# RWKV wave of a hybrid decoder step: fewer state DMAs, earlier loads, another order of the output groups, the last item and the last norms

## The chip, the cores and the metric

One core of one Trainium2 chip runs the whole step as one program. The metric is the device time of one execution in microseconds (us); the kernel before was run three times, and one further execution was profiled. Engines: PE (TensorE), ACT (ScalarE), DVE (VectorE), POOL (GpSimd) and SP (SyncE), which in this kernel issues every DMA.

## What is computed

Two layers for 1104 tokens (64 sample tokens in 8 sequences, 16 meta tokens, 1024 prompt tokens): a gated DeltaNet layer, which the change doesn't touch, then an RWKV-7 layer, a residual add and a final RMSNorm. The RWKV layer carries one state S per head (16 heads, 64 x 64) through the tokens:

```python
S = (S * d_t[:, :, None, :]
     + jnp.einsum('bhvk,bhk->bhv', S, -kk_t)[..., None] * b_t[:, :, None, :]
     + v_t[..., None] * k_t[:, :, None, :])
y_t = jnp.einsum('bhvk,bhk->bhv', S, r_t)
...
y = (y - mean) * lax.rsqrt(var + GN_EPS) * lnx_w + lnx_b      # per head
y = y + jnp.sum(r_h * k_h * r_k, -1, keepdims=True) * v_h
out = (y.reshape(B, T, D) * jax.nn.silu(z)) @ w_o
x = x + out                                                    # residual
y_out = rmsnorm(x, final_norm_w)
```

The eight sample sequences each start from a state of their own (`state_rwkv`) and return their new one (`s_rwkv`); the prompt's last state is `p_rwkv`.

## The kernel before, in words

Everything up to the wave is done by 1836 us: the DeltaNet layer, the RWKV projections, and the inverse "systems" of each chunk, written to DRAM (`ttd`).

The **wave** (lines 1864 to 1981) works on 24 **items**: 3 segments of 384, 384 and 336 tokens times 8 head pairs; item n is segment n // 8, pair n % 8, and has six chunks of 64 tokens. Step `tau` of the wave runs chunk `tau - 2n` of each live item n, so three items are in flight, one enters every two steps, and item n occupies steps 2n to 2n + 5. A step is: `step_solve` (PE products with the states, then the ACT copy `X`, line 1499, which opens the step in the profile's views here), `step_inner` (PE products with the system tile `rTT`, then two ACT copies), `step_old`, `step_state` (PE updates `rS` and `rY`, DVE writes the state), `y_stats`. PE and ACT run in the order in which the program writes their instructions (`manual_schedule`); DVE, POOL and SP are ordered by the planner of the framework, each in one queue.

Between these, a step places other work, by hand:
- **Front** of a coming item (`rwkv_front`): its loads at step 2n - 5 (`fld2c`, `fldrv`, `AR`, `BK`, lines 1254, 1364, 1365), its decays at 2n - 4, a third stage at 2n - 3 (`begun`), and six parts (scores, bonus, keys, values) at steps 2n - 2 and 2n - 1. The load of its system (`system`, line 1360) is in the fifth part, in step 2n - 1; it goes to one of three `rTT` tiles.
- **Sample states**, in segment 0 alone: `rwkv_sample_read` loads a pair's eight states by 8 DMAs (line 1608), and `rwkv_sample_write` makes the new ones in three stages (`ue`; the matmul `rsw` and two DVE updates; transposes and 8 DMAs out, line 1656).
- **Finish** of an item (`rwkv_finish`): group norm statistics, a square root by POOL and DVE, the ACT normalisation of six chunks (line 1578), transposes, gating, and the split of the result into a high and a low part (`yh`, `yl`), which the output projection needs. It advances in step 2n + 6, twice in 2n + 7, and in 2n + 8.
- **Fill**: lists of jobs with a number of units and a start and end in steps (lines 1893 to 1897); `fill(now)` runs units until the job is on its schedule. The jobs are the gate tiles, seven output groups (`out`, segment and range of pairs; each has eight blocks of 128 output columns), and the norms of segments 0 and 1 (`norms`); after the last step come group 5's and 6's rest and the last norms (`finish`).

The weights of the fill jobs come as a **stream** (line 217): a DMA to one of two raw tiles `wraw` (line 204), an ACT cast to `whi` and a POOL subtraction to `wlo` (lines 86 and 90), three of each, requested five tiles ahead of use. Output groups 0 to 4 read the running sums from DRAM (`x1T` to `zst`, line 1666), add, and write them back (line 1682); groups 5 and 6 add into tiles `x2` that stay on the chip (`sums_in`, line 1689), from which `finish` transposes, squares (ACT), takes the square root (POOL, DVE) and multiplies by the norm weight (DVE, line 1716).

Of the kernel before, what the change touches and what calls it, by code (L numbers as in the profile page):

```python
# [35 lines left out]
class Builder:  # L36
# [158 lines left out]
    def load_w(self, src, kt=8, into=None, later=False):  # L195
# [3 lines left out]
        v = src.rearrange("(k p) m -> p k m", p=128)  # L199
# [1149 lines left out]
    def rwkv_front(self, p, s):  # L1349
# [9 lines left out]
        def system():  # L1359
            nc.sync.dma_start(P.TT.rearrange("p c k -> p (c k)"), self.ttd[(P.n + 1) // 5][:, 384 * (P.n - max(5 * ((P.n + 1) // 5) - 1, 0)):][:, 0:384])  # L1360
# [19 lines left out]

        pr = t(fp, [128, 384], "pr", 1)
# [53 lines left out]
        P.parts = [[lambda: scores(0)], [bonus], [lambda: keys(0)], [lambda: scores(3)], [system, values], [lambda: keys(3)]]  # L1435
# [126 lines left out]
    def rwkv_finish(self, p, s, P):  # L1562
# [37 lines left out]
    def rwkv_sample_read(self, P):  # L1600
# [5 lines left out]
        for u in (0, 1):  # L1606
            for g in range(4):
                nc.sync.dma_start(sn[64 * u:64 * u + 64, g], st[u][:, g, 2 * p:2 * p + 2, :])
# [24 lines left out]
    def rwkv_sample_write(self, p, P, BT, DC):  # L1633
# [20 lines left out]
        for u in (0, 1):  # L1654
            for g in range(4):
                nc.sync.dma_start(st[u][:, g, 2 * p:2 * p + 2, :], so[64 * u:64 * u + 64, g])  # L1656


    def project_out(self, s, yo, pairs, tag, ws, x2=None):
# [3 lines left out]
        for ft in range(8):  # L1663
# [3 lines left out]
            w = next(ws)  # L1667
# [4 lines left out]
            for k, q in enumerate(pairs):  # L1672
                wh, wl = (x[:, k % 4] for x in w)
# [11 lines left out]
    def sums_in(self, s):  # L1685
        c0, n = SEGS[s]
        x2 = [self.t(self.fin2, [128, 384], "x2", 8) for ft in range(8)]
        for ft, x in enumerate(x2):
# [3 lines left out]
    def finish(self, s, x2):  # L1692
        nc, t, i, o, fp = self.nc, self.t, self.i, self.o, self.fin
        for q in range(3):
# [4 lines left out]
            r2 = t(self.fin2, [128, 2], "fr2", 2)  # L1699
            junk = t(self.fin2, [128, 512], "f2k", 3)  # L1700
# [4 lines left out]
            r, rs = t(self.fin2, [128, 1], "fr", 2), t(self.fin2, [128, 1], "frs", 2)  # L1705
            nc.vector.tensor_tensor(r[0:nr], r2[0:nr, 0:1], r2[0:nr, 1:2], op=ALU.add)
            nc.vector.tensor_scalar(r[0:nr], r[0:nr], 1.0 / D, RMS_EPS, op0=ALU.mult, op1=ALU.add)
            newton = self.rsqrt(rs[0:nr], r[0:nr], self.fin2, "fn", later=True)
# [13 lines left out]
            yield  # L1722

# [100 lines left out]
    def layer1(self, ctx, right, stay, xa, xb, x):  # L1824
# [31 lines left out]
        self.TTz = [t(ap, [128, 6, 64], f"rTT{q}") for q in range(3)]  # L1856
# [7 lines left out]
    def wave(self, zin, stay, last, pool):  # L1864
# [4 lines left out]
        P, x2 = {}, []  # L1869
# [4 lines left out]
                         [wo[128 * a:128 * b, 128 * k:128 * k + 128] for _, a, b in outs for k in range(8)])  # L1874

        def out(n, tag, x=None):
            s, a, b = outs[n]
            return self.project_out(s, [P[8 * s + q].out for q in range(a, b)], range(a, b), tag, ws, x)
# [8 lines left out]
        def norms(s):  # L1887
            x = self.sums_in(s)
            yield
            yield  # L1890
# [6 lines left out]
        more = [(lambda: norms(0), 8, 31, 36), (lambda: norms(1), 8, 47, 51), (lambda: x2.extend(self.sums_in(2)) or iter(()), 1, 51.6, 52)]  # L1897
# [35 lines left out]
        for tau in range(-3, 55):  # L1933
# [78 lines left out]
```

## Time and profile before

| | |
|---|---|
| median of 3 runs | 2326.65 us (2324.69 to 2329.08) |
| profiled execution, its own time | 2324.47 us |
| its span | 2322.5 us |
| granted clock of TensorE, mean | 0.968 |
| wave: step 1 opens | 1881.66 us |
| wave: step 51, the last, opens | 2273.00 us |
| DMA, over the span | 293.36 MB in 433127 packets, 148329 of them under 512 B |

The profile is one execution taken by the hardware profiler. Busy time per engine is summed over instructions; "idle before" names what ended an engine's idle time; the chain follows the last instruction back from releaser to releaser. A line number can be a helper's: 76, 80 and 73 are matmuls and transposes, 62 ACT, 86 and 90 the split. Tiles are named by the program's tags: `do` and `zo` are output groups in PSUM, `rX`, `rY` and `rS` the step's, `dsn`, `drsr`, `drsw` and `dsbT` the sample states'.

### The profile page before, as it was taken

What the parts mean: (1) busy time and instruction counts of PE and PEld (TensorE: products, weight loads), DVE (VectorE), ACT (ScalarE), POOL (GpSimd) and SP (SyncE); (2) the same over time, 40 slices, a digit from 0 to 9 for tenths busy, and PEclk for the clock granted to TensorE, in tenths of its full rate; (3) what the DMA queues carried; (4) which work ended last, traced back from release to release, by engine and by line L of the source; (5) the groups of instructions that cost most, each with busy time, mean ns of one, the idle gap of its engine ahead of it and who ended that gap; (6) DMA issues with size and microseconds to landing.
All of it is one profiled execution on the core that took longest, in us unless ns stands there. A gap on an engine that the chain in (4) does not pass through costs nothing. (4 is left out here: it accounts for less than half of the span.)

```text
span 2322.5 us, 55260 instructions
## 1 busy us (share of the span) xinstructions
PE 2144.8 (92%) x20452; PEld 1955.3 (84%) x20452; DVE 1594.6 (69%) x4224; ACT 1271.5 (55%) x3642; POOL 924.5 (40%) x1267
## 2 busy tenths in 40 slices
PE   6989999999999999999999989998889998999995
PEld 5888988989898888988999989888878976788874
DVE  6868768686768778695335765878978355767754
ACT  5445556455555556466433554746645355677763
POOL 3435344343434334444241442544434343444433
PEclk9999999999999999999999999998989999999998
DMA  3323333323334333427244146654552554677753
GB/s 115 100 76 107 80 89 87 109 66 92 95 89 114 85 87 81 113 70 209 69 125 117 61 114 206 197 187 143 166 144 80 176 140 131 184 226 230 223 149 119
DMA packets 433127, 293.36 MB, mean 126 GB/s; under 512 B 148329, under 2 KB 415706, under 8 KB 432858
## 3 DMA queue, kind: packets, MB, share of 16 engines
q1 hardware_dynamic: 432858, 289.84, 43.5%
q8 instruction: 161, 2.64, 0.5%
q14 instruction: 108, 0.88, 0.1%
HBM read 198.02 MB, written 91.71 MB: 125 GB/s over the span
## 5 line engine op out<-in xcount | busy, mean ns | idle before, releaser
L90 POOL TENSOR_TENSOR wlo<-wraw,whi 128x512 fp32r<-128x512 f32 (+2 forms) x252 | 328.2, 1305 | 363.3 <-ACT whi L86 347.3
L76 PE MATMUL d<-xc,whi 128*128 128x384 f32 (+2 forms) x910 | 263.0, 345 | 7.0 <-DVE key L1187 2.1
L86 ACT CAST whi<-wraw 128x512 fp32r<-128x512 f32 (+2 forms) x252 | 151.8, 604 | 115.7 <-PE dq L76 50.5
L434 DVE SCALAR_TENSOR_TENSOR cvy<-raw,cw,cvy 128x408 f32<-128x408 f32 (+2 forms) x288 | 179.3, 636 | 17.6 <-ACT cvy L62 15.8
L76 PEld LDWEIGHTS d<-xc,whi 128*128 128x128 f32 (+1 forms) x910 | 170.7, 194 | 14.4 <-issue 3.8
L472 DVE TENSOR_TENSOR invT<-invT,invtmp 72x31 f32<-72x31 f32 (+31 forms) x403 | 173.1, 430 | 6.7
L470 DVE TENSOR_TENSOR invtmp<-invA,invT 72x31 f32<-72x31 f32 (+31 forms) x403 | 165.4, 410 | 11.9 <-DMA invA<-ltd 5.1
L76 PE MATMUL dz<-xc,whi 128*128 128x384 f32 (+1 forms) x480 | 148.3, 340 | 0.0
L76 PE MATMUL dv<-xc,whi 128*128 128x384 f32 (+1 forms) x480 | 146.7, 335 | 0.0
L76 PE MATMUL d<-xc,wlo 128*128 128x384 f32 (+2 forms) x428 | 145.6, 346 | 0.5 <-POOL wlo L90 0.5
L76 PE MATMUL d<-xa,whi 128*128 128x384 f32 (+3 forms) x450 | 140.4, 345 | 2.3 <-DVE key L1187 0.9
L834 POOL TENSOR_SCALAR Sb<-Sb,eglb 128x128 f32<-128x128 f32 x128 | 80.5, 646 | 91.6 <-DMA Sb<-in_state_gdn 23.1
L76 PE MATMUL dv<-xa,whi 128*128 128x384 f32 (+1 forms) x288 | 100.0, 347 | 0.1
L76 PE MATMUL dz<-xa,whi 128*128 128x384 f32 (+1 forms) x288 | 99.6, 346 | 0.0
L76 PEld LDWEIGHTS d<-xa,whi 128*128 128x128 f32 (+1 forms) x450 | 83.9, 191 | 6.8 <-issue 2.4
L76 PEld LDWEIGHTS dz<-xc,whi 128*128 128x128 f32 x480 | 88.7, 190 | 0.8
L76 PEld LDWEIGHTS dv<-xc,whi 128*128 128x128 f32 x480 | 88.5, 188 | 0.5 <-issue 0.4
L76 PE MATMUL d<-xh,wlo 128*128 128x384 f32 (+1 forms) x256 | 85.1, 346 | 2.0 <-POOL wlo L90 2.0
L62 ACT ACTIVATE o<-rA,gcol 128x128 f32<-128x128 f32 x128 | 46.7, 372 | 73.3 <-DVE S L745 72.8
L76 PE MATMUL d<-xl,whi 128*128 128x384 f32 (+1 forms) x256 | 84.9, 347 | 1.9 <-DVE xl L90 1.3
L76 PE MATMUL d<-xh,whi 128*128 128x384 f32 (+1 forms) x256 | 85.3, 346 | 0.4 <-ACT xh L86 0.2
L76 PE MATMUL d<-xa,wlo 128*128 128x384 f32 (+3 forms) x252 | 85.4, 339 | 0.0
(512 smaller groups left out, 6986.8 us busy)
## 6 DMA issues: line engine op xcount, KB each, us to landing
wraw<-in_gdn_w_in SPq DMA_DIRECT2D x96, 256.0 KB
wraw<-in_rwkv_w_rkvz SPq DMA_DIRECT2D x80, 256.0 KB
Sb<-in_state_gdn SPq DMA_DIRECT2D x64, 256.0 KB
sldcak<-cakd SPq DMA_DIRECT2D x24, 576.0 KB
cakd<-ev SPq DMA_DIRECT2D x56, 192.0 KB
wraw<-in_rwkv_w_o SPq DMA_DIRECT2D x40, 256.0 KB
E<-drow SPq DMA_DIRECT2D x24, 384.0 KB
attn<-drow SPq DMA_DIRECT2D x24, 384.0 KB
```

The lines of the kernel that those rows point to most:

```text
L62: return self.nc.scalar.activation(out, in_, func, bias=bias, scale=scale, **kw)
L76: self.nc.tensor.matmul(out, lhsT, rhs, start=start, stop=stop)
L86: nc.scalar.copy(hi, x)
L90: e.tensor_tensor(lo, x, hi.bitcast(F32), op=ALU.subtract)
L434: nc.vector.scalar_tensor_tensor(y[:, 0:wd], raw[:, k:k + wd], cw[k], y[:, 0:wd], op0=ALU.mult, op1=ALU.add)
L470: nc.vector.tensor_tensor(tmp, A[:, j, j + 1:32].unsqueeze(2).broadcast_to([nb, n, m]), Tv[:, j, 0:m].unsqueeze(1).broadcast_to([nb, n, m] ...
L472: nc.vector.tensor_tensor(Tv[:, j + 1:32, 0:m], Tv[:, j + 1:32, 0:m], tmp, op=ALU.subtract)
L834: nc.gpsimd.tensor_scalar(Sb[:, u], Sb[:, u], self.eglb[:, hv, 4 * g + u:4 * g + u + 1], None, op0=ALU.mult)
```

## The change

- The sample states of a pair are read by 4 DMAs and written by 4: each moves one head of the pair for one half of the 64 partitions' rows, four groups of 64 values per partition instead of two.
- The system's DMA is moved from the fifth part (step 2n - 1) to the third stage of the front (step 2n - 3), ahead of the bonus products and of the sample read; there are four `rTT` tiles.
- The stream requests six tiles ahead, and every third raw tile is one of its own in another pool. Group 6's weights (one pair) come as two tiles of 128 x 512 instead of eight of 128 x 128.
- In a step, the finish that ends an item (the split) comes ahead of the one that normalises the next item; the sample write's stages come ahead of the front's third stage and of the fill (`ue`, transposes and DMAs out) and right after `step_state` (the matmul `rsw`).
- Item 23 normalises all six chunks in step 52, after the fill there, and splits at the end of step 53.
- Group 4 is cut in two: six blocks over steps 46 to 52, and two at 52.1 which add into `x2` tiles loaded earlier. Groups 5 and 6 are spread to 54.5 and 56. The norms of segment 1 begin at 46.3 instead of 47.
- The last norms (`finish_last`) do all transposes first, square with a scratch tile of their own (`f2s`), and give one half of two of the three row blocks to ACT (scaling) and POOL (multiplication); the rest stays on DVE.

```diff
-    def load_w(self, src, kt=8, into=None, later=False):
+    def load_w(self, src, kt=8, into=None, later=False, pool=None):
...
-            w = self.t(self.wp, [128, 4, 128], "wraw", 2)
-            m = min(4, kt - h)
+            w = self.t(self.wp if pool is None else pool, [128, 4, 128], "wraw", 2 if pool is None else 1)
+            m, n = (min(4, kt - h), n) if n <= 128 else (n // 128, 128)
...
-            while len(raw) < min(n + 5, len(srcs)):
+            while len(raw) < min(n + 6, len(srcs)):
                 q = len(raw)
-                if q > 1 and len(w) < q - 1:
+                if q > 2 and len(w) < q - 2:
...
-                raw.append(self.load_w(srcs[q], srcs[q].shape[0] // 128, later=True))
+                raw.append(self.load_w(srcs[q], srcs[q].shape[0] // 128, later=True, pool=self.fin if q % 3 == 2 else None))
...
-        def system():
-            nc.sync.dma_start(P.TT..., self.ttd...)
...
         yield P
+        nc.sync.dma_start(P.TT..., self.ttd...)
         pr = t(fp, [128, 384], "pr", 1)
...
-        P.parts = [..., [lambda: scores(3)], [system, values], [lambda: keys(3)]]
+        P.parts = [..., [lambda: scores(3)], [values], [lambda: keys(3)]]
...
-            if q in (3, 5):
+            if q == 5 or q == 3 and P.n < 23:
                 yield
...
-            for g in range(4):
-                nc.sync.dma_start(sn[64 * u:64 * u + 64, g], st[u][:, g, 2 * p:2 * p + 2, :])
+            for h in (0, 1):
+                nc.sync.dma_start(sn[64 * u:64 * u + 64, :, h], st[u][:, :, 2 * p + h, :])
...
+    def finish_last(self, x2):
...
+        def squares(q):
+            n = nr(q)
+            for h in (0, 1):
+                self.act(t(self.fin2, [128, 512], "f2s", 1)[0:n], ps[q][h][0:n], AF.Square, accum=r2[q][0:n, h:h + 1])
...
+                if h and q < 2:
+                    self.act(y[0:n], ps[q][h][0:n], AF.Identity, scale=rs[q][0:n])
+                    nc.gpsimd.tensor_tensor(y[0:n], y[0:n], self.fw[0:n, hs], op=ALU.mult)
+                else:
+                    nc.vector.scalar_tensor_tensor(y[0:n], ps[q][h][0:n], rs[q][0:n], self.fw[0:n, hs], op0=ALU.mult, op1=ALU.mult)
...
+        squares(0)
+        squares(1)
+        rows(0)
+        squares(2)
+        rows(1)
+        rows(2)
...
-        self.TTz = [t(ap, [128, 6, 64], f"rTT{q}") for q in range(3)]
+        self.TTz = [t(ap, [128, 6, 64], f"rTT{q}") for q in range(4)]
...
-                (lambda: out(2, Z), 16, 30, 38), (lambda: out(3, DD), 16, 38, 46), (lambda: out(4, Z), 16, 46, 51),
-                (lambda: out(5, DD, x2), 16, 52.1, 54), (lambda: out(6, DD, x2), 8, 54.1, 55), (lambda: self.finish(2, x2), 4, 55, 56)]
+                (lambda: out(2, Z), 16, 30, 38), (lambda: out(3, DD), 16, 38, 46), (lambda: out(4, Z, None, range(6)), 12, 46, 52), (lambda: out(4, DD, x2, (6, 7)), 4, 52.1, 52.45),
+                (lambda: out(5, DD, x2), 16, 52.1, 54.5), (lambda: out(6, DD, x2), 8, 54.6, 56), (lambda: self.finish_last(x2), 1, 56, 57)]
...
-                if 0 <= (tau - 6) // 2 < 24:
-                    next(P[(tau - 6) // 2].done)
-                for f in begun:
-                    next(f)
-                begun.clear()
                 if tau % 2 == 0 and 0 <= (tau - 8) // 2 < 24:
                     next(P[(tau - 8) // 2].done, None)
-                fill(tau + 0.5)
-                for f in parts[1]:
-                    f()
+                if 0 <= (tau - 6) // 2 < 24 and tau != 52:
+                    next(P[(tau - 6) // 2].done)
                 for Q, ci in items:
                     if ci == 1 and Q.s == 0:
                         late.append(self.rwkv_sample_write(Q.p, Q, Q.BT, Q.DC))
                 late = [x for x in late if not next(x, True)]
+                for f in begun:
+                    next(f)
+                begun.clear()
+                fill(tau + 0.5)
+                if tau == 52:
+                    next(P[23].done)
+                for f in parts[1]:
+                    f()
                 if W:
                     self.step_state(W)
+                late = [x for x in late if not next(x, True)]
                 fill(tau + 1)
                 for f in parts[2]:
                     f()
-                late = [x for x in late if not next(x, True)]
...
```

More of the change, by code (lines that the diff above doesn't have):

```diff
@@ L1379, in rwkv_front @@
         yield P
+        nc.sync.dma_start(P.TT.rearrange("p c k -> p (c k)"), self.ttd[(P.n + 1) // 5][:, 384 * (P.n - max(5 * ((P.n + 1) // 5) - 1, 0)):][:, 0:384])
         pr = t(fp, [128, 384], "pr", 1)
@@ L1434, in values @@
                     u += m
[L1435 removed]
+        P.parts = [[lambda: scores(0)], [bonus], [lambda: keys(0)], [lambda: scores(3)], [values], [lambda: keys(3)]]
         if s == 0:
@@ L1666, in project_out @@
                 nc.sync.dma_start(x[:, 0:n], self.x1T[ft][:, c0:c0 + n])
-            w = next(ws)
+            w = next(ws) if len(pairs) > 1 or ft % 4 == 0 else w
             x = x if x2 is None else x2[ft]
@@ L1672, in project_out @@
             for k, q in enumerate(pairs):
-                wh, wl = (x[:, k % 4] for x in w)
+                wh, wl = (x[:, k % 4 if len(pairs) > 1 else ft % 4] for x in w)
                 yh, yl = yo[k]
@@ L1683, in project_out, with sums_in @@
             yield
-    def sums_in(self, s):
+    def sums_in(self, s, fts=range(8)):
         c0, n = SEGS[s]
-        x2 = [self.t(self.fin2, [128, 384], "x2", 8) for ft in range(8)]
-        for ft, x in enumerate(x2):
+        x2 = {ft: self.t(self.fin2, [128, 384], "x2", 8) for ft in fts}
+        for ft, x in x2.items():
             self.nc.sync.dma_start(x[:, 0:n], self.x1T[ft][:, c0:c0 + n])
@@ L1698, in finish @@
             ps = [self.ps(*tag, "fin"), self.ps(*tag, "fin")]
-            r2 = t(self.fin2, [128, 2], "fr2", 2)
-            junk = t(self.fin2, [128, 512], "f2k", 3)
+            r2 = t(self.fin2, [128, 2], "fr2", 3)
+            junk = t(self.fin2, [128, 512], "f2s", 1)
             for h in (0, 1):
@@ L1967, in wave @@
                     f()
-                late = [x for x in late if not next(x, True)]
                 if tau % 2 and 0 <= (tau - 7) // 2 < 24:
-                    next(P[(tau - 7) // 2].done)
+                    next(P[(tau - 7) // 2].done, None)
                 if W:
```

52 lines of the change are left out of this document (37 added, 15 removed).

## The prediction

> **What bounds the kernel now.** I read the page first, then busy time by stage, then by step, then the waits and the chain inside the stages that stand out.
>
> ```profile
> PE 2144.8 (92%) x20452; PEld 1955.3 (84%) x20452; DVE 1594.6 (69%) x4224; ACT 1271.5 (55%) x3642; POOL 924.5 (40%) x1267
> ```
>
> TensorE is busy for 92% of the span, so only the stages where it idles can give time. The changed code is the RWKV wave. The view by stretches has duration, then PE, weight load, DVE, ACT, POOL busy with counts, granted clock, DMA share, GB/s. I cut at the ACT copies that open each step `tau` (line 1499; the first, at 1881.66, is step 1), so the rows are: all before the wave, its entry, steps 1 to 4, 5 to 14, 15 to 45, 46 to 50, and the tail from step 51.
>
> ```profile
> 0.00:1836.00 1836.00, 1714.12 (x14374) 1587.40 (x14375) 1299.82 (x3225) 983.28 (x2800) 725.29 (x1031) 0.97 0.39 112
> 1836.00:1881.66 45.66, 40.98 (x292) 38.06 (x290) 16.45 (x37) 15.96 (x35) 20.88 (x38) 0.93 0.76 223
> 1881.66:1909.66 28.00, 26.80 (x390) 22.46 (x389) 19.82 (x61) 16.23 (x48) 11.81 (x15) 1.00 0.51 140
> 1909.66:2004.83 95.17, 82.72 (x1253) 68.49 (x1251) 62.32 (x210) 53.31 (x156) 36.01 (x42) 0.95 0.53 146
> 2004.83:2233.72 228.89, 219.72 (x3564) 187.49 (x3560) 156.41 (x564) 165.24 (x494) 98.87 (x108) 1.00 0.71 212
> 2233.72:2273.00 39.28, 33.08 (x411) 28.09 (x411) 19.60 (x72) 23.02 (x73) 16.39 (x16) 0.96 0.56 170
> 2273.00:2322.50 49.50, 27.38 (x182) 23.32 (x182) 20.17 (x58) 14.43 (x45) 15.20 (x21) 0.82 0.31 98
> ```
>
> The change touches nothing in the first 1836 us. In the rest PE idles 12.5 us in steps 5 to 14, 9.2 in 15 to 45, 6.2 in 46 to 50, 22.1 in the tail, 4.7 at the entry. That is 55 us, plus what a lowered clock costs. It is the pot; the question is how much of it this change opens. Single steps, same view:
>
> ```profile
> 1919.47:1931.33 11.86, 8.43 (x87) 7.33 (x89) 5.39 (x19) 5.71 (x16) 1.28 (x2) 0.71 0.58 167
> 1997.34:2004.83 7.49, 7.09 (x97) 5.97 (x97) 5.25 (x17) 5.61 (x17) 3.48 (x4) 1.00 0.96 297
> 2057.84:2065.65 7.81, 7.13 (x105) 5.70 (x107) 4.65 (x19) 5.46 (x16) 3.02 (x4) 1.00 0.53 150
> 2065.65:2072.78 7.13, 7.08 (x128) 6.14 (x125) 5.04 (x18) 4.92 (x16) 3.47 (x5) 1.00 0.70 199
> 2072.78:2079.37 6.59, 6.59 (x105) 5.74 (x107) 4.56 (x19) 5.47 (x17) 2.56 (x3) 1.00 0.71 207
> 2233.72:2244.84 11.12, 8.63 (x97) 7.28 (x97) 3.17 (x16) 4.99 (x15) 3.87 (x4) 0.85 0.58 167
> ```
>
> A clean pair of late steps is 7.13 + 6.59 = 13.7 us and full of PE work. Step 6 takes 11.86, step 46 11.12.
>
> **Part 1: state DMAs 8+8 to 4+4, system load two steps earlier, sample update sooner (steps 5 to 14).** The SyncE queue ahead of step 6 (its issues in order, time, duration, count), a line of the chain, the issue durations by line (min/median/max ns), and who PE waited for in the wave (total us, times, longest):
>
> ```profile
> 1907.81 6.47 SPq L1656 DMA_DIRECT2D out_s_rwkv<-ssn  x8
> 1914.38 0.54 SPq L204 DMA_DIRECT2D wraw<-in_rwkv_w_rkvz  x1
> 1914.96 5.63 SPq L1608 DMA_DIRECT2D sn<-in_state_rwkv  x7
> 1920.70 0.54 SPq L1360 DMA_DIRECT2D rTT<-ttd  x1
> ```
> ```profile
> L1608 SPq DMA_DIRECT2D sn<-in_state_rwkv x64: 597/606/1680, 1853.9 to 1977.1; - x64
> L1365 SPq DMA_DIRECT2D BK<-abd x22: 370/388/2147, 1875.3 to 2203.0; - x22
> ```
> ```profile
> PE rX L80 <- DMA rTT<-ttd: 6.3, 6, 3.1
> PE drsw L76 <- DVE xss L1631: 5.5, 7, 1.1
> ```
> ```profile
> SPq L1608 <- PE dsn L73: 7.9, 3, 3.4
> ```
>
> The system for the item that enters at step 6 is issued at 1920.70, behind 15 sample DMAs that held the queue 12.1 us, and step 6 waits for it. An item (two steps, here about 20 us) costs 16 x 0.61 = 9.8 us of queue. The change leaves 8 issues. What one of them costs is not in the trace: it moves 256 runs of 256 B where 128 went before. Bounds: 0.39 us (line 1365, 768 such runs, cheaper than 128 are now) and 1.2 (twice the present). Line 1365 says that runs don't set the price, so I take 0.61: 4.9 us saved per item. With the upper end nothing is saved. The bytes are unchanged.
>
> The system load moves from half a step ahead of its use to two and a half, in front of the state reads, and needs the fourth tile because its tile is free only after that step's inner solve. So the 6.3 us of PE waits go. Cost if the cover fails: the issue waits on PE and holds the queue; the nearest such hold is line 1608 on PE, up to 3.4 us. I take 0, since its tile has just been freed where it is placed.
>
> The sample write's matmul moves ahead of the fill and of the third read stage. Its wait for the PSUM buffer (5.5 us) goes; the read stage's second buffer now waits for VectorE's update of the sample state instead, with a fill unit between them; behind it on PE stand the finish transposes and the next step's solve. Bounds: minus 5.5 and plus 5.5; I take minus 3.
>
> Sum. PE is busy 82.7 of 95.2 us, at clock 0.95: about 78 at full clock. Clean steps run at 1 to 4% of idle; with two leftovers I take 83, so **minus 12 us**, bounds minus 17 (all idle and clock) and minus 5 (only the PE waits on the system).
>
> The Trainium skill's "DMA: Bandwidth & Descriptors", section "Issuing engines are not separate DMA queues", says that the sequencer's time to initiate a DMA is usually small relative to the DMA itself; by it, halving the issues would bring nothing and this part would give 0. The rows above show 12.1 us of issue in a row with PE waiting behind, so I go by the rows and keep that as a rival.
>
> **Part 2: weights one load further, third raw buffer (entry, tail).** At the entry one weight transfer keeps PE waiting:
>
> ```profile
> 1857.25 3.13 DMA wraw<-in_rwkv_w_rkvz
> PE zz L76 <- DVE zst L1003: 3.4, 1, 3.4
> ```
>
> Ahead of it in the queue stand state reads, now half. Bounds 0 and minus 6 (the wait, and the slow clock after it: 0.93 over the entry); I take **minus 3**.
>
> **Part 3: finish steps reordered (15 to 50).** Now, ACT normalises the next item (line 1578) before it splits the finished one that the output group needs:
>
> ```profile
> 2235.99 1.42 ACT L62 ACTIVATE y<-y,gnm,grs 128x64 f32<-128x64 f32 x4
> 2237.31 0.46 ACT L86 CAST yh<-lz 128x336 fp32r<-128x336 f32 x1
> 2237.82 0.42 PE L76 MATMUL zo<-yh,whi 128*128 128x336 f32 x1 [1.54 <-ACT yh L86]
> ```
>
> With the order swapped the split starts 1.42 us sooner at steps 14, 22, 30, 38 and 46. Steps 22, 30 and 38 are 7.81 (row above) against some 7.1: up to 0.7 each. The waits of PE on the system in steps 17 to 45 go too:
>
> ```profile
> PE rX L80 <- DMA rTT<-ttd: 1.4, 3, 0.8
> ```
>
> Together 3 x 0.7 + 1.4 = 3.5, and a little at steps 14 to 16, where sample DMAs still fill the queue: **minus 4** for steps 15 to 45, bounds minus 1 and minus 8 (nearly all idle time).
>
> Step 46 gains most: group 4 starts with one unit instead of two ahead of the state matmuls, so these no longer stand behind the split. Two of its eight blocks (24 matmuls, 3.7 us) leave steps 46 to 50 altogether, and the norms of segment 1 begin earlier. I take step 46 from 11.1 to 7, and 2 us from the rest: **minus 6**, bounds minus 2 and minus 9.
>
> About 1.7 of that is the clock, 0.85 in this step after a PE wait of 1.54 us. The skill's "TensorE: Matmul & The Clock Gate", Part 1, lets the clock fall after at least one idle window of about 3.4 us; by that rule the slow stretch has another cause and stays, and the term would be minus 4.3. The row shows the fall after a shorter wait.
>
> **Part 4: the tail.** The step's rest, the PE wait, matmul pitch, splits, weight transfers, norms:
>
> ```profile
> 2274.41 0.98 PE L76 MATMUL fyT<-ident,y 64*64 64x64 f32 x24
> 2281.84 0.65 PE L76 MATMUL do<-yh,whi 128*128 128x336 f32 x1 [4.44 <-ACT yh L86]
> 2288.30 0.31 PE L76 MATMUL do<-yh,whi 128*128 128x336 f32 x1
> 2288.45 0.32 PE L76 MATMUL do<-yl,whi 128*128 128x336 f32 x1
> 2307.09 1.70 PE L73 MATMUL dfin<-ident,x 128*128 128x128 f32 x8
> 2314.92 0.59 ACT L62 ACTIVATE f2k<-rfin 80x512 f32<-80x512 f32 x1 [3.88 <-DMA out_y_prompt<-f2k]
> 2317.97 1.41 DVE L1716 SCALAR_TENSOR_TENSOR f2k<-rfin,frs,fw 80x512 f32<-80x512 f32 x2
> ```
> ```profile
> 2290.02 2.88 DMA wraw<-in_rwkv_w_o
> 2294.62 2.10 DMA wraw<-in_rwkv_w_o
> ```
> ```profile
> L90 POOL TENSOR_TENSOR wlo<-wraw,whi 128x384 fp32r<-128x384 f32 x7 | 7.1, 1007 | 5.8 <-ACT whi L86 4.7 <-PE do L76 1.1
> L86 ACT CAST whi<-wraw 128x384 fp32r<-128x384 f32 x7 | 3.6, 512 | 7.9 <-PE do L76 5.0 <-DMA wraw<-in_rwkv_w_o 2.9
> ```
>
> Now: PE waits 4.44 us for the split, then runs slow, then with two raw buffers gets a weight tile every 2 us or so (two tiles per transfer of 2.1 to 2.9 us and a split of 0.5 + 1.0) where 9 matmuls need 1.4.
>
> After: up to 2275.4 as now (2.4 us after 2273.0). Then 24 matmuls of group 4 stand where PE waited, 72 of group 5 and 24 of group 6: 120 x 0.155 = 18.6. The last item's transposes add 1.2. Three raw buffers make (2.9 + 1.5)/3 = 1.5 us per tile, just over the 1.4; group 6 needs two 512-wide tiles instead of eight. I allow 1.5 for waits. Its last item splits one stage sooner, under group 5. So the last group ends 2.4 + 18.6 + 1.2 + 1.5 = 23.7 us after 2273.0; now it ends at 34.1.
>
> Then the norms, now 15.4 (2307.1 to 2322.5). The squares get their own scratch, so the 3.88 us wait for an output transfer goes; the scratch is single, in ACT's order anyhow. In the new order ACT has 6 squares and 2 scalings of 0.6, VectorE 4 multiplies of 0.7 instead of 6, GpSimd two multiplies (not in the trace; between the 1.0 of a 384-wide split and 1.7, I take 1.3). Last result 9 to 10.4 us after the group's end, and 3.1 from there to the end as now: 12.8. Tail 36.5 instead of 49.5: **minus 13**, bounds minus 8 (weights still bind) and minus 16.
>
> **Sum.** 3 + 12 + 4 + 6 + 13 = 38 us. The profiled execution took 2324.47 (span 2322.5, 2.0 around it): 2286.5. The median shown, 2326.65, lies 2.2 higher: 2288.6, said as **2289**. About 0.2% (4.7 us) is what a measurement can tell from no change.
>
> **Rivals.**
> - *The issues were not the limit.* Transfers, VectorE's sample update or the new PSUM wait take over in steps 5 to 14: 0 instead of 12, 2301. For: DMA share reaches 0.96 in step 14, and VectorE is busy 65%. Against: mean share 0.53. Chance 0.17.
> - *The tail stays bound by weights.* 8 weight tiles still go through one queue behind the sum reads: minus 5 there, 2297. For: 1.5 against 1.4 us leaves no slack. Chance 0.14.
> - *All stalls close.* Upper bounds at entry and in steps 5 to 14, and some of the others: minus 50, 2277. Chance 0.08.
> - *Slower.* The earlier system load sits in the queue until PE has freed its tile, with the front's loads and the weights behind it, in each of 24 items. At 3.4 us (the longest such hold) it costs 82, net plus 44: 2371. It decides from 38/24 = 1.6 us an item. Against: one hold that long in the wave now. Chance 0.06.
> - *It does not do what it says.* The load order on SyncE is the planner's; if it leaves the loads late and the queue as full, gains and new waits cancel: within 0.2%. Chance 0.03.
>
> The forecast itself (29 to 48 us saved) gets 0.52. **Range** 2274 to 2310: gains of 17 to 53 us; it leaves out the last two rivals and the ends of the others. **Chances**: faster 0.91, same 0.03, slower 0.06.
>
> **What would show it.** Steps 5 to 14 near 83 us, no PE wait on the system load, line 1608 and 1656 with 32 issues each near 0.6 us. Step 46 under 8 us. In the tail no PE wait over 2 us ahead of group 5, the last group ending some 24 us after step 51's copy, and no wait of ACT for an output transfer. Wrong if issues take twice as long, if SyncE waits on PE at the system load, or if PE in the tail waits for weight splits at each block.

## The result, and the profile after

The changed kernel takes **2296.41 us** in the median (2294.90 to 2297.98, 4 runs); the kernel before, run beside it on the same chip, 2325.67 (2321.49 to 2329.08). The ratio is 0.9869, 95% interval 0.9847 to 0.9892: faster by 1.1 to 1.5%. Forecast were 2289 us and 38 us saved; 29 came. The profiled execution took 2294.90 us, span 2293.2.

Read the same stages first, cut at the same ACT copies (columns as before: duration, PE, weight load, DVE, ACT, POOL, clock, DMA share, GB/s):

```profile
0.00:1841.82 1841.82, 1722.94 (x14374) 1596.69 (x14375) 1301.35 (x3225) 982.91 (x2800) 724.08 (x1031) 0.97 0.39 112
1841.82:1887.09 45.27, 41.11 (x292) 38.19 (x291) 16.43 (x37) 15.72 (x36) 20.83 (x38) 0.92 0.80 236
1887.09:1913.62 26.53, 26.53 (x390) 21.86 (x389) 20.06 (x61) 16.31 (x47) 11.35 (x15) 1.00 0.61 158
1913.62:1992.84 79.22, 77.19 (x1253) 64.14 (x1251) 61.33 (x212) 53.01 (x156) 37.59 (x42) 1.00 0.62 174
1992.84:2220.37 227.53, 219.18 (x3564) 189.35 (x3560) 153.68 (x563) 165.08 (x493) 99.04 (x109) 0.98 0.73 211
2220.37:2250.82 30.45, 26.01 (x375) 20.96 (x375) 17.50 (x76) 21.68 (x70) 12.90 (x13) 1.00 0.60 185
2250.82:2293.20 42.38, 29.25 (x218) 26.29 (x218) 20.63 (x52) 15.65 (x43) 20.47 (x20) 0.88 0.37 115
```

The first row speaks of no edit: up to there both kernels issue the same instructions in the same order on every engine, and yet the last store of the systems, which ends the row, is issued here at 1841.82 us and in the profile of before at 1835.94:

```profile
1835.94 0.78 SPq L1344 DMA_DIRECT2D ttd<-sTD  x2
```
```profile
1841.82 0.78 SPq L1344 DMA_DIRECT2D ttd<-sTD  x2
```

I call this issue the **marker**. In the executions below it lies anywhere from 1832.85 to 1843.01 us. So one execution's span says little about a few us; a stage's own length says much, since most steps that no edit touches repeat within 0.02 us from kernel to kernel. From the marker on, the change saves 486.6 - 451.4 = 35.2 us:

| stage | before | after | change | forecast |
|---|---|---|---|---|
| entry, marker to step 1 | 45.7 | 45.3 | -0.4 | -3 |
| steps 1 to 4 | 28.0 | 26.5 | -1.5 | - |
| steps 5 to 14 | 95.2 | 79.2 | -16.0 | -12 |
| steps 15 to 45 | 228.9 | 227.5 | -1.4 | -4 |
| steps 46 to 50 | 39.3 | 30.5 | -8.8 | -6 |
| tail | 49.5 | 42.4 | -7.1 | -13 |

In steps 5 to 14 PE now idles 2.0 us instead of 12.5. The issues of the sample states, by line (min/median/max ns), are half as many and cost the same each, though each now moves 256 runs of 256 B:

```profile
L1607 SPq DMA_DIRECT2D sn<-in_state_rwkv x32: 601/614/2022, 1860.6 to 1958.4; - x32
```
```profile
L1655 SPq DMA_DIRECT2D out_s_rwkv<-ssn x32: 607/615/1680, 1896.3 to 2010.5; - x32
```

Steps 15 to 45 hide a loss. Step by step they are shorter than before or equal, except step 34, 14.77 us (8.78 before), and step 31, 8.20 (7.12). Step 34, on VectorE and then PE:

```profile
2122.68 1.41 DVE L1715 SCALAR_TENSOR_TENSOR f2k<-dfin,frs,fw 128x512 f32<-128x512 f32 x2
2129.03 0.75 DVE L1715 SCALAR_TENSOR_TENSOR f2k<-dfin,frs,fw 128x512 f32<-128x512 f32 x1
2133.32 0.75 DVE L1715 SCALAR_TENSOR_TENSOR f2k<-dfin,frs,fw 128x512 f32<-128x512 f32 x1 [3.54 <-DMA out_y_prompt<-f2k]
2133.99 1.01 DVE L1408 TENSOR_TENSOR G<-fG,gm 128x384 f32<-128x384 f32 x2
```
```profile
2134.59 0.69 PE L76 MATMUL fbonus<-prh,bones 128*128 128x384 f32 x1 [4.09 <-DVE G L1408]
```

The first two rows `f2k` were done by 2124.1, but SyncE issued nothing from 2123.3 to 2126.2, and sent them only at 2129.35:

```profile
2122.88 0.38 SPq L1362 DMA_DIRECT2D AR<-abd  x1
2126.20 0.32 SPq L1665 DMA_DIRECT2D zst<-x1T  x1
2126.57 0.42 SPq L1379 DMA_DIRECT2D rTT<-ttd  x1
2127.09 1.54 SPq L1254 DMA_DIRECT2D fld2c<-cakd  x1
2128.73 0.53 SPq L1254 DMA_DIRECT2D fldrv<-rvd  x1
2129.35 0.56 SPq L1717 DMA_DIRECT2D out_y_sample<-f2k  x1
```

SyncE's largest wait from the marker to the end, and its wait at the moved system load (total us, times, longest):

```profile
SPq L1665 <- DMA x1T<-zst: 92.6, 34, 6.0
SPq L1379 <- PE rS L80: 2.2, 4, 1.1
```

The first is the read of a sum into one of the two `zst` tiles, whose last contents have to be written out first; it is not new (69.0 us in 32 waits before), but has grown. The second, the moved system load, is small: with two other waits of 0.8 us it comes to 3.0 us behind PE, against 3.8 at its old place in the kernel before. A third hold has grown a little: the sample reads (line 1607) wait 20.5 us for PE in six waits, the longest 6.0 (before 16.4 in seven, 3.4); with 2.0 us of idle PE in steps 5 to 14 it cost PE next to nothing there. In step 34 the queue held on a sum's read, the outputs stood behind it, the fourth row waited for a buffer of three, the scores `G` of a coming item stood behind that row on VectorE, and PE behind the scores. This is a stall of the norms, not of the wave's own work.

### The profile page after: what moved, and what is told of

It reads as the page before. It is cut to its first block, busy times and chain, and to the rows that moved or that the text cites. A ratio compares the mean times of both kernels' runs of the same rounds, so it can differ in the third digit from the quotient of the medians.

```text
span 2293.2 us, 55145 instructions
## 1 busy us (share of the span) xinstructions
PE 2142.2 (93%) x20452; PEld 1957.5 (85%) x20452; DVE 1591.0 (69%) x4222; ACT 1270.4 (55%) x3638; POOL 926.3 (40%) x1263
## 5 line engine op out<-in xcount | busy, mean ns | idle before, releaser
L90 POOL TENSOR_TENSOR wlo<-wraw,whi 128x512 fp32r<-128x512 f32 (+1 forms) x246 | 325.5, 1326 | 379.1 <-ACT whi L86 366.9
L86 ACT CAST whi<-wraw 128x512 fp32r<-128x512 f32 (+1 forms) x246 | 150.2, 613 | 105.1 <-PE dq L76 50.6
L834 POOL TENSOR_SCALAR Sb<-Sb,eglb 128x128 f32<-128x128 f32 x128 | 80.1, 643 | 88.2 <-DMA Sb<-in_state_gdn 43.8
L62 ACT ACTIVATE attn<-attn,gcol 128x128 f32<-128x128 f32 x144 | 46.5, 390 | 70.2 <-POOL attn L545 70.1
```

Of the source, the lines that this page charges most:

```text
L62: return self.nc.scalar.activation(out, in_, func, bias=bias, scale=scale, **kw)
L86: nc.scalar.copy(hi, x)
L90: e.tensor_tensor(lo, x, hi.bitcast(F32), op=ALU.subtract)
L834: nc.gpsimd.tensor_scalar(Sb[:, u], Sb[:, u], self.eglb[:, hv, 4 * g + u:4 * g + u + 1], None, op0=ALU.mult)
```

## The experiments

In all of them 8+8 means eight DMAs that read and eight that write an item's sample states, 4+4 four of each. One execution of each kernel was profiled: times of steps and stages come from it, the time of the whole is the median of its runs. Theories at the start. **T**: in steps 5 to 14 the issue time of the sample states on SyncE was the limit; the half count freed it. **Rival A**: the place of the system load did it. **Rival B**: the order of the sample update did. For step 34: the buffer, or SyncE's order whatever the buffers. For the tail: weights, order of the last groups, or the norms.

**State DMAs back to 8+8.**
```diff
-            for h in (0, 1):
-                nc.sync.dma_start(sn[64 * u:64 * u + 64, :, h], st[u][:, :, 2 * p + h, :])
+            for g in range(4):
+                nc.sync.dma_start(sn[64 * u:64 * u + 64, g], st[u][:, g, 2 * p:2 * p + 2, :])
```
(and the write likewise)

> The changed kernel with the sample states read and written by 8+8 DMAs again; system load, sample update and the rest stay changed. Changed kernel for comparison: steps 5 to 14 take 79.2 us, 15 to 45 227.5, median 2296.4. Theory (the issue time of the state DMAs on SyncE holds steps 5 to 14): the issues of 0.61 us double to 16 per item, steps 5 to 14 go back to 88 to 93 us, the whole to 2305 to 2310. Rival A (it was the place of the system load, which no longer stands behind the state DMAs): steps 5 to 14 stay under 82.5 us, the whole under 2300. Rival B (it was the earlier sample update): the same as A here, told apart by the next two runs.

Measured: 2309.17 us, ratio to before 0.9919 (0.9891 to 0.9948). The time of the whole is as T said; where it is lost isn't. Steps 5 to 14 took 82.7 us where 88 to 93 were expected; steps 17 and 19 took 10.5 and 12.7 us (7.1 and 7.4 in the changed kernel).

**System load back in its old place**: the DMA goes from the third stage of the front back into the fifth part, four tiles stay.
```diff
-        P.parts = [..., [values], [lambda: keys(3)]]
+        P.parts = [..., [system, values], [lambda: keys(3)]]
```

> The changed kernel with the system load moved back to its old place, half a step ahead of its use; 4+4 DMAs and four tiles stay. Theory (issue time): with half as many state issues ahead of it the load is no longer late, steps 5 to 14 stay at 79 to 82 us and the whole at 2296 to 2299. Rival A (place of the system load): PE waits on rTT come back (6.3 us in steps 5 to 14 before, plus the slow clock behind them), steps 5 to 14 at 85 to 92 us, the whole at 2302 to 2309, and 1 to 2 us more in steps 15 to 45.

Measured: 2295.60 us, 0.9854 (0.9819 to 0.9890); steps 5 to 14 79.2. With 4+4 DMAs and the new orders the place is worth nothing there: rival A is out for this kernel.

**Before, with 4+4 alone**: the first diff the other way round, in the kernel before.

> The kernel before with only the sample states' DMAs changed to 4+4. Theory (issue time): steps 5 to 14 fall from 95.2 us to 83 to 87, the other stages stay, the whole falls by 8 to 12 us. Rival A (place of the system load): steps 5 to 14 above 91 us, the whole less than 4 us below. Rival B (place of the sample update): steps 5 to 14 keep their PE waits on the sample update's VectorE copies (5.5 us) and come to 87 to 90, the whole 5 to 8 us below.

Measured: 2313.99 us, 0.9944 (0.9924 to 0.9963); steps 5 to 14 84.9, which is T's figure; step 6 fell from 11.86 to 6.2. One system load was still late, in step 20:

```profile
2038.52 0.27 PE L80 MATMUL rX<-X,rTT 64*64 64x64 f32 x1 [2.21 <-DMA rTT<-ttd]
```

**Both undone**: 8+8 DMAs and the old place of the load.

> The changed kernel with 8+8 state DMAs and the system load in its old place at once. Known so far: steps 5 to 14 take 79.2 us in the changed kernel, 82.7 with 8+8 alone undone, 79.2 with the place of the load alone undone, 95.2 in the kernel before. Theory now (a full SyncE queue is the limit, and either edit alone frees the system load from it): with both undone PE waits for systems again, steps 5 to 14 come to 86 to 91 us and the whole to 2310 to 2318. Rival (the place of the load is worth nothing even behind a full queue; the rest of the gain is the order of the sample update and the finish steps): steps 5 to 14 stay at 82 to 84 us as with 8+8 alone, the whole at 2306 to 2310.

Measured: 2304.54 us, 0.9904 (0.9880 to 0.9927); steps 5 to 14 81.8. My theory of two edits that replace each other fell: even behind the full queue the place of the load costs nothing in these steps. But steps 17 and 19 took 14.2 and 13.1 us. SyncE and VectorE ahead of step 19's wait, then PE's waits in both steps (this kernel's line numbers are two higher):

```profile
2008.21 5.62 SPq L1657 DMA_DIRECT2D out_s_rwkv<-ssn  x8
...
2018.43 1.68 SPq L1667 DMA_DIRECT2D zst<-x1T  x1
```
```profile
2025.84 0.56 DVE L1681 TENSOR_TENSOR zst<-zst,zo 128x384 f32<-128x384 f32 x1 [4.98 <-DMA zst<-x1T]
```
```profile
2007.44 0.69 PE L76 MATMUL zo<-yh,whi 128*128 128x384 f32 x1 [3.92 <-DVE zst L1681]
2026.45 0.45 PE L76 MATMUL zo<-yh,whi 128*128 128x384 f32 x1 [2.10 <-DVE zst L1681]
```

The eight writes hold the queue for 5.6 us, the sum's read follows eight other issues later, VectorE waits for it, and PE for VectorE, which has yet to empty the one PSUM buffer of the group. Step 17 is the same one item earlier: eight writes from 1989.47, the read at 2000.90, VectorE's wait until 2006.83. The late issue is not all of it: VectorE has the data of step 19's read only 7.4 us after it is issued (2018.43 to 2025.84).

**Old order of the sample update**: its three stages back behind the fill and the read stages.
```diff
-                for Q, ci in items:
...
-                late = [x for x in late if not next(x, True)]
                 for f in begun:
...
                 for f in parts[1]:
                     f()
+                for Q, ci in items:
...
+                late = [x for x in late if not next(x, True)]
```
(and the second call back behind `parts[2]`)

> The changed kernel with the sample states' update (its products, the update's matmuls, its write) back in its old places in each step. The kernel before with 4+4 DMAs alone took 84.9 us for steps 5 to 14, the changed one 79.2, so 5.7 us belong to the other edits. Theory (the order of the sample update gives most of them, as PE no longer waits for a PSUM buffer held by VectorE's copies): steps 5 to 14 at 82 to 85 us, later steps unchanged, the whole at 2298 to 2302. Rival (the finish order gives them): steps 5 to 14 below 80.5.

Measured: 2298.15 us, 0.9882 (0.9857 to 0.9908); steps 5 to 14 83.4, steps 1 to 4 28.0 as before. So this order gives 4.2 of the 5.7 us in steps 5 to 14: rival B holds for most of the rest of the gain. Steps 1 to 20 of all these kernels, in us:

| kernel | 1 to 4 | 5 to 14 | 15 to 20 | sum |
|---|---|---|---|---|
| before | 28.0 | 95.2 | 45.8 | 168.9 |
| before, 4+4 alone | 28.0 | 84.9 | 46.7 | 159.5 |
| changed | 26.5 | 79.2 | 42.5 | 148.2 |
| 8+8 | 28.4 | 82.7 | 52.4 | 163.5 |
| old place of load | 26.5 | 79.2 | 43.8 | 149.5 |
| 8+8 and old place | 26.9 | 81.8 | 56.7 | 165.4 |
| old sample order | 28.0 | 83.4 | 43.1 | 154.5 |

Half the issues are worth 9.4 us in the old kernel and 15 to 16 in the new, the sample order 6.2, the place of the load at most 2. Part of the 15 to 16 may be chance: step 19 took 10.8 and 10.9 us in two later kernels with 4+4 as well (7.4 in the changed one), so up to 3.5 us of it need no eight issues; step 17 was over 7.5 us only with 8+8. By the medians, each as its ratio to the kernel before, half the issues are worth 12 to 13 us. The single terms don't add. My reading, which no run here isolates: a queue that is behind is paid for wherever PE next catches up with it, and the faster steps 5 to 14 left the eight-issue queue less time, so that the bill came in steps 17 and 19.

**Four buffers `f2k`** instead of three.

> The changed kernel with four buffers instead of three for the normalised output rows f2k. In the changed kernel step 34 takes 14.8 us (8.8 before), with VectorE waiting 3.5 us for an output transfer of f2k. Theory (that buffer is what holds step 34, as PE waits for scores queued behind it on VectorE): step 34 comes down to 8 to 10 us, steps 15 to 45 from 227.5 to 222 to 223 us, the whole to about 2291. Rival (SyncE's order is late whatever the buffers, and the wait goes to the next transfer in the queue): step 34 stays above 12 us, the whole within 2 us of 2296.

Measured: 2289.27 us, 0.9849 (0.9811 to 0.9887); step 34 8.79 us, PE's wait ahead of the same matmul 0.46 us although SyncE's outputs came just as late (6.9 us after the rows were begun; 6.7 in the changed kernel):

```profile
2125.57 0.45 PE L76 MATMUL fbonus<-prh,bones 128*128 128x384 f32 x1 [0.46 <-DVE G L1408]
```

So the buffer held the step. Over all profiled executions: with three buffers step 34 took 11.1 to 16.7 us in nine of ten kernels with the changed loop or 4+4 DMAs (8.8 in the tenth, below), with four 8.8 in three of three. The rest of the expected gain did not show, since step 19 took 10.8 us in this execution (7.4), again a late sum read; steps 15 to 45 took 224.9.

**Old finish order**: the next item is normalised ahead of the split.
```diff
+                if 0 <= (tau - 6) // 2 < 24 and tau != 52:
+                    next(P[(tau - 6) // 2].done)
                 if tau % 2 == 0 and 0 <= (tau - 8) // 2 < 24:
                     next(P[(tau - 8) // 2].done, None)
-                if 0 <= (tau - 6) // 2 < 24 and tau != 52:
-                    next(P[(tau - 6) // 2].done)
```

> The changed kernel with the old order of the two finish stages in a step: the next item is normalised before the finished one is split. Theory (ACT's 1.4 us of normalising ahead of the split delays the first output unit of a group): steps 22, 30 and 38 go from 6.6 back to 7.8 us each, step 46 from 5.4 to 6.5 to 8, steps 5 to 14 up by 0 to 2, the whole up by 4 to 7 to about 2302. Rival (in these steps the state matmuls or the group's first transfer end last): steps 22, 30 and 38 stay below 7, step 46 below 6, the whole within 2 us.

Measured: 2293.24 us, 0.9851 (0.9828 to 0.9874). Steps 22, 30, 38 took 7.81, 7.82, 7.81 us as before (6.61, 6.61, 6.60 in the changed kernel), step 14 0.7 more, step 46 1.3, step 48 1.1, the tail 1.3: 8 us, each step as the theory says. The whole was not: about 2302 was expected, and it did not rise. In the profiled execution step 34 took 8.78 us, 6.0 less than in the changed kernel: its sums' reads fell otherwise, and the outputs went out 1.9 us after the rows were begun instead of 6.7. From the marker it comes to 452.2 us against 451.4. So the order gains 8 us in the stages that it touches and, by chance, met a stall of 6 in another; whether the runs that were not profiled had step 34 the same is not known.

**Two raw weight tiles**, five loads ahead.

> The changed kernel with two raw weight buffers and one load less of lookahead, as before; the two 512-wide tiles of the last group stay. Tail (from the X copy of step 51): 42.4 us in the changed kernel, 49.5 before. Theory (weight tiles arrive in pairs every 4 us or so with two buffers, where 9 matmuls take 1.4 us a tile): PE waits at several blocks of group 5, the tail is 46 to 49 us, the entry up by 0 to 2, the whole 2300 to 2304. Rival (the two blocks of group 4 put in front of group 5 give the loads time enough): tail below 43.5, the whole below 2298.

Measured: 2297.34 us, 0.9880 (0.9855 to 0.9905); tail 48.5 us, 6.1 longer, with PE waiting for splits of weights and of the last item; from the marker 458.5, 7.2 longer. The whole stayed below 2298, which was the rival's figure. Two of the waits:

```profile
2256.11 0.42 PE L76 MATMUL do<-yh,whi 128*128 128x336 f32 x1 [1.08 <-ACT whi L86]
2271.30 0.42 PE L76 MATMUL do<-yl,whi 128*128 128x336 f32 x1 [1.40 <-POOL yl L90]
```

The medians are only 0.9 us apart and don't show it: in the profiled executions this kernel's marker lay 8.9 us earlier than that of the changed one, more than the whole effect, and the medians may carry such differences too. The third tile also has a price in the wave: with two, steps 7 and 11 take 8.8 and 9.3 us instead of 10.2 and 10.3, while step 29 takes 11.1 instead of 7.2.

One more thing is in this execution. The wait ahead of step 51's products is 1.94 us as in the changed kernel, but the matmuls behind it start every 0.15 us, at a granted clock of 1.00:

```profile
2243.28 0.27 PE L80 MATMUL rX<-X,rTT 64*64 64x64 f32 x1 [1.94 <-ACT X L1498]
...
2245.31 0.32 PE L76 MATMUL zo<-yl,whi 128*128 128x336 f32 x1
2245.47 0.32 PE L76 MATMUL zo<-yh,wlo 128*128 128x336 f32 x1
```

In the changed kernel the same matmuls start every 0.28 us (rows under the last combination), and its granted clock from the X copy to the transposes is 0.70. So there the transposes come 4.2 us after the copy, here 3.15.

**Group 4 in one piece** in steps 46 to 50.
```diff
-(lambda: out(4, Z, None, range(6)), 12, 46, 52), (lambda: out(4, DD, x2, (6, 7)), 4, 52.1, 52.45),
+(lambda: out(4, Z), 16, 46, 51),
...
```
(and the loads of the sums moved to fit)

> The changed kernel with output group 4 in one piece of 16 units in steps 46 to 50, as before; the finish order, weights and norms stay changed. Changed kernel: steps 46 to 50 30.5 us, tail 42.4, together 72.8; before 39.3 and 49.5. Theory (24 matmuls, 3.7 us, go back into steps 46 to 50, and PE waits 3 to 4.5 us again for the split ahead of group 5): steps 46 to 50 at 34 to 37, tail at 41 to 44, together 76 to 80. Rival (moving the two blocks only shifts the same work, the wait was already short by the finish order): together 72 to 74.

Measured: 2298.54 us, 0.9871 (0.9834 to 0.9907); steps 46 to 50 37.4, tail 38.2, together 75.6 against 72.8: between the two expectations. Moving two blocks is worth 2.8 us, less than thought; the wait ahead of group 5 is now short without them (1.9 us in two pieces, 4.44 before):

```profile
2264.31 0.42 PE L76 MATMUL do<-yh,whi 128*128 128x336 f32 x1 [0.78 <-ACT yh L86]
2265.86 0.56 PE L76 MATMUL do<-yl,whi 128*128 128x336 f32 x1 [1.12 <-POOL yl L90]
```

**Last norms on VectorE alone.**
```diff
-                if h and q < 2:
+                if False:
```
In the changed kernel, GpSimd and VectorE in the last norms:

```profile
2283.64 1.27 POOL L1753 TENSOR_TENSOR f2k<-f2k,fw 128x512 f32<-128x512 f32 x1
2286.80 1.26 POOL L1753 TENSOR_TENSOR f2k<-f2k,fw 128x512 f32<-128x512 f32 x1
```
```profile
2282.38 0.16 DVE L111 SCALAR_TENSOR_TENSOR fn_t<-fn_t,fr 128x1 f32<-128x1 f32 x1
2283.81 1.11 DVE L111 SCALAR_TENSOR_TENSOR fn_t<-fn_t,fr 128x1 f32<-128x1 f32 x1
2286.87 1.21 DVE L110 TENSOR_TENSOR fn_t<-frs 80x1 f32<-80x1 f32 x1 [0.65 <-POOL frs L102]
```

The same operation on one column takes 0.16 us, or ends within 0.02 us of the GpSimd multiply beside it (2284.92 and 2284.91; 2288.08 and 2288.06).

> The changed kernel with all six multiplies of the last norms on VectorE (no GpSimd multiply, no scaling on ACT). In the changed kernel two VectorE operations on one column take 1.11 and 1.21 us instead of 0.16, each beside a GpSimd multiply of 1.27 us; the norms take 14.2 us from their first transpose to the end of the span. Theory (VectorE is held while GpSimd multiplies): no such operation above 0.3 us, the norms at 12.2 to 13.2 us although VectorE does two more multiplies of 0.75, the tail 1 to 2 us shorter than 42.4. Rival (the sharing was worth it, the two multiplies queue on VectorE and the output buffers bind): norms at 14 to 15 us.

Measured: 2291.08 us, 0.9840 (0.9806 to 0.9875). The norms took 12.7 us (2270.50 to 2283.2) instead of 14.2, and no such operation took more than 0.16:

```profile
2275.92 0.16 DVE L111 SCALAR_TENSOR_TENSOR fn_t<-fn_t,fr 128x1 f32<-128x1 f32 x1
2277.05 0.14 DVE L110 TENSOR_TENSOR fn_t<-frs 80x1 f32<-80x1 f32 x1
```

The run takes away ACT's two scalings together with GpSimd's multiplies, so the 1.5 us is the price of the sharing as a whole.

**A combination**: four row buffers, norms on VectorE, two raw tiles until the last groups, item 22 normalised behind the X copy of step 51, item 23's low part split on VectorE, the last group's sums over four PSUM buffers.
```diff
-                if 0 <= (tau - 6) // 2 < 24 and tau != 52:
+                if 0 <= (tau - 6) // 2 < 24 and tau not in (50, 52):
                     next(P[(tau - 6) // 2].done)
+                if tau == 51:
+                    next(P[22].done)
...
```
(the part for item 22; the other edits are small and are left out here)

> A combination on top of the changed kernel: four output-row buffers; the last norms on VectorE alone; two raw weight buffers in the wave and the third only for the last groups; the normalising of item 22 put into step 51 behind the X copy; item 23's low part split on VectorE; the last group's sums over four PSUM buffers. If the findings so far hold: step 34 at 8.8 us (minus 6 against the profile of the changed kernel), steps 5 to 14 at 76.7 (minus 2.5), step 51's X copy without ACT's normalising ahead and no half clock behind it (minus 2 to 3), one PE wait of 1 us in the last group less, norms minus 1.5: tail at 36 to 38.5, the whole at 2281 to 2288. If the waits only move on: tail above 40, the whole above 2290.

Measured: 2281.95 us, 0.9818 (0.9776 to 0.9861): the whole, step 34 (8.79) and steps 5 to 14 (76.7) as hoped, the tail (41.6 us) as in the other case. Step 29 took 11.1 us with fewer weights ahead.

**The combination with the weights as in the changed kernel.**

> The combination without its edit to the weights (third raw buffer and six loads ahead throughout, as in the changed kernel). In the first combination step 29 took 11.1 us (7.2 in the changed kernel) and group 5 waited three times for weight splits, so that the tail from step 51's copy was 41.6 us; both were seen only with fewer weights ahead. Theory (the weights were what ate the gain): step 29 back at 7.2, steps 7 and 11 back at 10.2 and 10.3, no PE wait over 0.5 us on a weight split in group 5, tail at 36.5 to 38.5, the span from the marker before the wave (the last store of the triangular systems) at 443 to 445.5 us, the whole at 2279 to 2286. Rival (group 5 waits for weights in any order that reaches it earlier): tail at 40 or more, from the marker 447 or more.

Measured: **2280.72 us, 0.9806 (0.9776 to 0.9837)**, 1.9% under the kernel before. From the marker 442.7 us, 8.7 less than the changed kernel; but the tail is 41.5 us, and there the rival was right. Step 29 took 8.3, not 7.2; steps 7 and 11 took 10.2 and 10.3, as expected. In the last wave step the edit did its work: PE's wait for the X copy, 1.94 us in the changed kernel, is 0.30 (the changed kernel first, then this one):

```profile
2251.07 0.27 PE L80 MATMUL rX<-X,rTT 64*64 64x64 f32 x1 [1.94 <-ACT X L1498]
...
2253.49 0.48 PE L76 MATMUL zo<-yl,whi 128*128 128x336 f32 x1
2253.77 0.48 PE L76 MATMUL zo<-yh,wlo 128*128 128x336 f32 x1
```
```profile
2242.52 0.27 PE L80 MATMUL rX<-X,rTT 64*64 64x64 f32 x1 [0.30 <-ACT X L1498]
...
2244.56 0.32 PE L76 MATMUL zo<-yl,whi 128*128 128x336 f32 x1
2244.71 0.32 PE L76 MATMUL zo<-yh,wlo 128*128 128x336 f32 x1
```

After the long wait a matmul starts every 0.28 us, after the short one every 0.15. (With two raw tiles, above, it was 0.15 after the long wait too.) But group 5 then starts sooner than its weights: the weight load is issued behind the read of the last sum, which SyncE holds until the sum is written, and ACT waits 4.19 us for it and PE 1.12 for the split (SyncE, ACT, PE):

```profile
2248.61 0.38 SPq L1681 DMA_DIRECT2D x1T<-zst  x1
2251.92 0.32 SPq L1688 DMA_DIRECT2D x<-x1T  x1
2252.33 0.39 SPq L204 DMA_DIRECT2D wraw<-in_rwkv_w_o  x1
```
```profile
2255.10 0.51 ACT L86 CAST whi<-wraw 128x384 fp32r<-128x384 f32 x1 [4.19 <-DMA wraw<-in_rwkv_w_o]
```
```profile
2255.66 0.42 PE L76 MATMUL do<-yh,whi 128*128 128x336 f32 x1 [1.12 <-ACT whi L86]
```

## Why the prediction was right, and where it was off

- **State DMAs (part 1).** The step held: 256 runs cost no more to issue than 128 (0.61 us), half the issues are worth 9.4 to 16 us over steps 1 to 20, and 4+4 alone takes 10.3 off steps 5 to 14. The Trainium skill's "DMA: Bandwidth & Descriptors", section "Issuing engines are not separate DMA queues", which calls the time to initiate a DMA usually small, gives 0 for this as the prediction read it; the same bytes in twice the issues cost 15 us here (12 by the medians), so the rival built on it is out.
- **System load (part 1).** That its move takes PE's 6.3 us of waits away failed: with the move undone they stay away, even behind eight issues. In the old kernel the half count takes the wait in step 6 away by itself; with eight issues it was another of the edits, perhaps the sample order or the fourth tile, and no run tells which. The prediction also read the row too broadly: 4.8 of the 6.3 us lie in steps 5 to 14, the rest are the waits that part 3 counts as 1.4. The feared hold of SyncE at its new place (rival "slower") came to 3.0 us in six waits on PE in all, less than at the old place, and not 1.6 us an item.
- **Sample order (part 1).** The sign was right, the size 6.2 us for 3, of which 4.2 in steps 5 to 14. With the 10.3 of the state DMAs alone this is most of the 16 us where 12 were said.
- **Entry (part 2)**, -3 forecast, -0.4 measured. The step that failed is that one load further on request ends PE's wait: it is 3.16 us (3.37 before). PE waits there for a gate tile to be drained, which stands on ACT behind the cast of a coming weight tile, and ACT now waits 4.07 us for that tile's transfer (2.91 before). Why the transfer comes no sooner was not taken apart; the DMA share is 0.80 for 0.76. The executions of the other kernels have 43.6 to 46.4 us, so even the sign is open.
- **Finish order (part 3).** 1.2 us for each of steps 22, 30 and 38 where 0.7 was said, plus 4.4 elsewhere. The term of steps 15 to 45 was still missed, -1.4 for -4, by a step that the prediction lacked: it put nothing for the norms of segment 0, which run there, and counted the wait for a row buffer `f2k` only in the last norms, as gone. But these rows wait on SyncE's order. Step 34 took back 6.0 and step 31 1.1.
- **Steps 46 to 50 (part 3)**, -8.8 for -6: step 46 went to 5.4 us, not 7. Undone one at a time, the finish order costs 2.5 us here and the two blocks 7.0, of which the tail gets 4.2 back.
- **Tail (part 4)**, -7.1 for -13, the term that was most wrong in size. The third raw buffer works (6.1 us), but: the first six blocks of group 4 were still not done at step 51 and ran at half clock behind a wait that the prediction didn't have (the transposes that I put 1.4 us after the copy came at 4.2; at full clock, as with two raw tiles, 3.15); the last group ended 28.2 us after the copy, not 23.7; and GpSimd's multiplies, priced right (1.27 us for 1.3), held VectorE, and the norms took 14.2 and not 12.8. On VectorE alone they take 12.7.
- **The clock.** Behind step 51's wait of 1.94 us the clock fell (0.70 up to the transposes), and it did not fall in the combination without that wait (last rows above); step 46, at 0.85 before, has lost its slow stretch with its wait of 1.54 us, and steps 46 to 50 ran at 1.00. By the Trainium skill's "TensorE: Matmul & The Clock Gate", Part 1, the clock falls after an idle window of about 3.4 us, so these shorter waits would cost nothing. The measurement decides: a shorter wait can cost a slow stretch too. It need not: of the nine profiled executions with a wait of 1.93 to 1.99 us at step 51, eight ran at half clock behind it and one, with two raw tiles, did not. What tells them apart is open.
- **The sum.** 35 us from the marker for 38. That it is so near is partly luck: steps 5 to 14 and 46 to 50 gave 6.8 us more than forecast and steps 1 to 4 an unforecast 1.5, while entry, steps 15 to 45 and tail gave 11.1 less. Profile against profile 2286.5 us were forecast and 2294.90 measured; of these 8.4 us, 2.8 are the sum and 5.9 the stretch ahead of the marker, which no edit touches (0.3 the other way lie outside the span).

Left open is also what makes step 19 or 34 draw late sum reads in one kernel and not in another. SyncE's order comes from the planner, and I didn't fix that order by itself.

## What to carry to other kernels

Count the issues of a DMA queue per unit of work: here 0.61 us each with 128 runs or with 256, and with twice the issues the loss showed up steps later, where another load stood at the queue's end. Ask of every buffer that is written out how long the queue ahead of its output may hold, not how long the transfer takes. When the gains of several edits are to be told apart, compare stages between fixed marks and take each edit away from the whole as well as adding it alone.

## What the runs showed of the hardware that I had not expected

- VectorE operations on one column waited for a GpSimd multiply to end (1.11 and 1.21 us for 0.16). The Trainium skill's "SBUF — State Buffer", section "SBUF: two separate sides", says why: GpSimd and a VectorE operation with two inputs in SBUF share a port pair that is locked for a whole instruction. The trace agrees: both VectorE operations end within 0.02 us of the multiply.
- A stretch of some 1840 us with the same instructions in the same order took 1835.94 and 1841.82 us in two executions, while most steps of 7 us repeat to 0.02 us.
- The same wait of 1.94 us ahead of the same matmuls was followed by matmuls every 0.28 us in one kernel and every 0.15 us in another.
